# A two-layer decoder trunk on one core: two norm rows sent through DRAM on the GpSimd queue, and the last output block in two column halves

## The chip, the core and the metric

The kernel runs on one core of a Trainium2 chip. The time is the device time of one execution, in microseconds (us). Before the change it is 1134.34 us, the median of three runs (1133.87 to 1134.71).

## What is computed

A trunk of two layers over 512 tokens of width 1024, all in float32. Layer 0 mixes tokens by a forgetting attention (FoX), layer 1 by a latent attention (MLA) whose keys and values are computed from the stream after layer 0. Each layer ends in a squared-ReLU MLP of width 4096, and a last RMS norm closes the trunk:

```python
def rms_norm(x, g):
    y = x * lax.rsqrt(jnp.mean(x * x, axis=-1, keepdims=True) + EPS)
    return y * g

for layer in range(2):
    h = rms_norm(x, norm_mix_g[layer])
    x = x + (fox_mixer if layer == 0 else mla_mixer)(h, ...)
    h = rms_norm(x, norm_ffn_g[layer])
    x = x + jnp.square(jax.nn.relu(h @ w_up[layer])) @ w_down[layer]
    if layer == 0:
        k_nope, k_rope, v = mla_shared_kv(x, kv_norm_g, ...)
return rms_norm(x, final_norm_g)
```

## The kernel before, in words

**Tiling.** A stream `x` lies as 8 tiles of 128 features by 512 tokens. To keep float32 accuracy on TensorE, each operand is split into a high and a low part (`split`: ScalarE casts `hi`, VectorE subtracts to get `lo`) and each product is three matmuls (`three`). Weights come in pieces of 128x1024: a load into `raw` on SyncE's queue, a cast to `whi` on ScalarE, a subtraction to `wlo` on VectorE. Almost every operation is recorded through one helper, so most rows of the profile say L112, and tiles tell them apart.

**Order.** In the stages that matter here, TensorE, VectorE and ScalarE each carry out their instructions in exactly the order in which the code writes them (`order["on"]`). GpSimd (POOL) is not in that list; it has its own in-order stream. In the two MLPs (`ffn`) a table sets the order: `at(step, rank, fn)` files each piece of work under a step, and the steps are emitted one after another, by rank within a step.

**The norm's rows.** The norm's factor for each token, 1/sqrt(mean square), is computed once for 128 tokens by 4 blocks: `token_sums` on TensorE, two integer steps on VectorE, twelve small ones on POOL (`rsqrt_of`, L327 to L330). Tokens then lie on partitions. Where features lie on partitions, the factor is needed as a row of 512 tokens that is the same on all 128 partitions. `along_tokens` makes this with four float32 matmuls against an identity (`x8` in the profile, since each of them shows as two), and `rstd_tile` (L341) copies the result out of PSUM on ScalarE into a tile `rstd`. This happens three times: in the FoX stage (which the change leaves alone), in layer 0's MLP (`row`, L756, put at step 3; used only for the last 8 of 32 hidden blocks, `up_post`), and in MLA (L1158). There the row serves one multiplication, `u = krp * row` (L1165), whose result ScalarE rearranges (the two `copy` of 64 partitions at L1168). In ScalarE's order stand, behind these copies, the squares of the key-value latents (`square`, L1171 and L1176), whose sum over features is the next norm's `token_sums` (L1190) and, behind that, the chain of small VectorE steps `rsqrt_of(..., alone=True)` (L1194).

**The end.** The last MLP writes its output with tokens on partitions: for each of 4 blocks of 128 tokens and each of two halves of 512 features (`o`), `block_mm` (L1332) accumulates 24 matmuls in one PSUM bank; then the bank is scaled and added to the stream `xtok` (`add_to`, one VectorE operation). `o = 1` is done first for all blocks; when `o = 0` is added, `finish` (L1296) closes the block: the sum of squares on ScalarE (`activation` with `accum_out`), one VectorE operation that adds the two halves' sums, two integer operations and three Newton steps of two operations each on a 128x1 column (`fs`), and then both halves are scaled (`t` on VectorE, `u` on ScalarE) and stored by the queues of SyncE and ScalarE. For the last block nothing is left that could hide this chain.

Of the kernel before, what the change touches and what calls it, by code (L numbers as in the profile page):

```python
# [97 lines left out]
def trunk(ctx: ExitStack, tc: tile.TileContext, xT, wts, gains, fing, rope, out):  # L98
# [63 lines left out]
    def tt(shape=(P, S)):  # L162
        return tp_.tile(list(shape), F32, tag="t", name=nm("t"))
# [150 lines left out]
    def rsqrt_of(v, mult=1.0, alone=False, tags=("rs1", "rs2")):  # L314
        y, a = (small.tile([P, v.shape[-1]], F32, tag=t, name=nm("rs"), bufs=2 if t[:2] == "rs" else 1) for t in tags)

        nc.vector.tensor_single_scalar(a.bitcast(I32), v.bitcast(I32), 1, op=ALU.arith_shift_right)
        nc.vector.tensor_scalar(y.bitcast(I32), a.bitcast(I32), -1, RSQRT_BITS, op0=ALU.mult, op1=ALU.add)
        for step in range(3):
            m = mult if step == 2 else 1.0  # L320
            if alone:
                nc.vector.tensor_tensor(a, y, y, op=ALU.mult)
                nc.vector.scalar_tensor_tensor(out=a, in0=a, scalar=-0.5 * m, in1=v, op0=ALU.mult, op1=ALU.mult)
                nc.vector.scalar_tensor_tensor(out=y, in0=a, scalar=1.5 * m, in1=y, op0=ALU.add, op1=ALU.mult)
            else:

                nc.gpsimd.tensor_tensor(a, y, y, op=ALU.mult)  # L327
                nc.gpsimd.tensor_tensor(a, a, v, op=ALU.mult)
                nc.gpsimd.tensor_scalar(a, a, -0.5 * m, 1.5 * m, op0=ALU.mult, op1=ALU.add)
                nc.gpsimd.tensor_tensor(y, a, y, op=ALU.mult)  # L330
        return y
# [9 lines left out]
    def rstd_tile(r, tag="tp"):  # L341
        rb = along_tokens(r, tag)
        t = small.tile([P, S], F32, tag="rstd", name=nm("rstd"), bufs=2)
        nc.scalar.copy(t, rb)
        return t

    class Filler:
# [321 lines left out]
    def ffn(acc, layer, tokens, tail, begin):  # L669
# [8 lines left out]
        with ExitStack() as fs:  # L678
# [75 lines left out]
                nc.gpsimd.tensor_tensor(r2, rs, rs, op=ALU.mult)  # L754

            def row():  # L756
                norm["row"] = rstd_tile(norm["rs"], "go")

            def up_post(n):
                hf, j = divmod(n, HALF // P)  # L760
# [257 lines left out]
    with ExitStack() as mx:  # L1018
# [136 lines left out]
        prepare(KA + 4)  # L1155
        low_rank(ql[1], w[2][:4], hm, 0)
        low_rank(ql[2], w[2][4:], hm, 0)
        row = rstd_tile(rs)  # L1158
        prepare(KA + 5)


# [109 lines left out]
    fpool = ctx.enter_context(tc.tile_pool(name="fin", bufs=1, reuse_waits="tile"))  # L1271
    gfin = fpool.tile([P, D], F32, name="gfin")
    nc.scalar.dma_start(gfin, fing.partition_broadcast(P))
    nc.gpsimd.tensor_scalar(gfin, gfin, -1.0 / 8192, 0.0, op0=ALU.mult, op1=ALU.add)
    sums = fpool.tile([P, 2, NB], F32, name="sums")

    def turn_stream(at):
# [11 lines left out]
    def finish_first(tb):  # L1289
# [3 lines left out]
        nc.vector.tensor_scalar(sums[:, 1, tb : tb + 1], sums[:, 1, tb : tb + 1], 1.0 / D, EPS, op0=ALU.mult, op1=ALU.add)  # L1293
        nc.vector.tensor_tensor(xtok[tb][1], xtok[tb][1], gfin[:, S:], op=ALU.mult)

    def finish(tb):  # L1296

        junk = tt()
        nc.scalar.activation(out=junk, in_=xtok[tb][0], func=AF.Square, accum_out=sums[:, 0, tb : tb + 1])
        v, a, y = (small.tile([P, 1], F32, tag=f"fs{j}", name=nm("fs"), bufs=2) for j in range(3))  # L1300
        nc.vector.tensor_scalar(v, sums[:, 0, tb : tb + 1], 1.0 / D, sums[:, 1, tb : tb + 1], op0=ALU.mult, op1=ALU.add)
        nc.vector.tensor_single_scalar(a.bitcast(I32), v.bitcast(I32), 1, op=ALU.arith_shift_right)
        nc.vector.tensor_scalar(y.bitcast(I32), a.bitcast(I32), -1, RSQRT_BITS, op0=ALU.mult, op1=ALU.add)

        for m in (3.0, 12.0, 768.0):
            nc.vector.scalar_tensor_tensor(out=a, in0=y, scalar=v, in1=y, op0=ALU.mult, op1=ALU.mult)
            nc.vector.scalar_tensor_tensor(out=y, in0=a, scalar=-m, in1=y, op0=ALU.add, op1=ALU.mult)
        t, u = tt(), tt()
        nc.scalar.activation(out=u, in_=xtok[tb][1], func=AF.Copy, scale=y)
        nc.vector.scalar_tensor_tensor(out=t, in0=xtok[tb][0], scalar=y, in1=gfin[:, :S], op0=ALU.mult, op1=ALU.mult)  # L1310
        nc.scalar.dma_start(out[tb * P : (tb + 1) * P, S:], u)
        nc.sync.dma_start(out[tb * P : (tb + 1) * P, :S], t)

    def by_tokens(e, after, at, fn):

        s, los, quads, quad, w_cast, w_low, combine, add_to = (fn[n] for n in ("s", "los", "quads", "quad", "w_cast", "w_low", "combine", "add_to"))
        sh, sl, dn, lows = {}, {}, {}, []

        def hidden(k):
            return s[2 * CHUNKS + k // 4][:, k % 4, :]  # L1320

        def cast(k):
            sh[k] = rt()
            nc.scalar.copy(sh[k], hidden(k))

        def low(k):
            if k % 4 == 0:
                lows.append(fn["sp"].tile([P, 4, S], F32R, tag="s", name=nm("sl")))
            sl[k] = lows[-1][:, k % 4, :]
            nc.vector.tensor_tensor(sl[k], hidden(k), f32(sh[k]), op=ALU.subtract)  # L1330

        def block_mm(tb, o):  # L1332
            dn[tb, o] = bank(("up", "up", "go", "go")[tb])
            t = slice(tb * P, (tb + 1) * P)
            for i in range(4):
                for j in range(2):

                    k = i // 2 * 4 + j * 2 + i % 2
                    three(dn[tb, o], *los["w", o, i][j], sh[k][:, t], sl[k][:, t], i == 0 and j == 0, i == 3 and j == 1, flip=True)

        for k in range(KD):
            at(after + 1 + k // 2, 5, cast, k)
            at(e - 3 + k // 3, 2.5, low, k)
        for o in range(2):
            for i in range(4):
                m = ("w", o, i)
                hf, a = 2 * CHUNKS + i // 2, i % 2
                src = lambda hf=hf, a=a, o=o: quads[hf, a, o]
                due = e - 5 + i if o else e - 1 + i
                at(due - 4, 9, quad, hf, a, o)  # L1350
                at(due, 6, w_cast, m, src, i % 2 == 0 if o else i == 0)
                at(due + 1, 3, w_low, m, src)
        for n, (o, tb) in enumerate((o, tb) for o in (1, 0) for tb in range(NB)):
            at(e + n, 0, block_mm, tb, o)
            at(e + n + 1, 1, lambda tb=tb, o=o: add_to(tb, o, dn[tb, o]))
            if o == 0:
                at(e + 4 + tb // 2, 4, finish_first, tb)
                at(e + n + 1, 3.5, finish, tb)
        for j, part in enumerate(("u2", "u3", "c11", "c21", "v", "c12", "u4", "c22")):
            for b in range(2):  # L1360
                at(e + j // 2, 4, combine, b, part)
# [111 lines left out]
```

## Time and profile before

| | before |
|---|---|
| median of 3 runs | 1134.34 us (1133.87 to 1134.71) |
| the profiled execution: its time | 1133.68 us |
| its span, first to last instruction | 1131.9 us |
| granted TensorE clock | 0.999 |
| layer 0's MLP | about 261 to 599 us |
| MLA, from its first matmul to its output projection | about 599 to 786 us |
| layer 1's MLP and the end | about 786 us to the end |

The time of a run is longer than its span by what lies around it, 1.78 us in the profiled execution. The profile has the busy time of each engine, the chain of work that ended last (followed back from the end, each step to what released it), a timeline of the instructions with their start, length and the idle time before them, and groups of instructions by shape. In an instruction's name the tile before the arrow is written and the ones behind it are read.

### The profile page before, as it was taken

What the parts mean: (1) busy time and instruction counts of PE and PEld (TensorE: products, weight loads), DVE (VectorE), ACT (ScalarE), POOL (GpSimd) and SP (SyncE); (2) the same over time, 40 slices, a digit from 0 to 9 for tenths busy, and PEclk for the clock granted to TensorE, in tenths of its full rate; (3) what the DMA queues carried; (4) which work ended last, traced back from release to release, by engine and by line L of the source; (5) the groups of instructions that cost most, each with busy time, mean ns of one, the idle gap of its engine ahead of it and who ended that gap; (6) DMA issues with size and microseconds to landing.
All of it is one profiled execution on the core that took longest, in us unless ns stands there. A gap on an engine that the chain in (4) does not pass through costs nothing.

```text
span 1131.9 us, 14269 instructions
## 1 busy us (share of the span) xinstructions
PE 1114.8 (98%) x5340; PEld 910.8 (80%) x5340; DVE 780.6 (69%) x1420; ACT 581.7 (51%) x1060; POOL 19.7 (2%) x71
## 2 busy tenths in 40 slices
PE   8999999999999999999999999999999999999997
PEld 6777887788888888888888777788888888888885
DVE  6797888764567677577885877737256765765784
ACT  5565655644555454444454666635465544444622
POOL 1000000001000000000001100000100000000000
PEclk9999999999999999999999999999999999999999
DMA  5322222143724315311244211313442511611402
GB/s 189 132 94 92 77 75 75 57 147 96 278 95 149 112 38 171 108 57 56 98 144 137 79 41 52 112 56 97 159 173 67 183 67 56 191 62 42 135 1 75
DMA packets 36822, 116.66 MB, mean 103 GB/s; under 512 B 4224, under 2 KB 4864, under 8 KB 36752
## 3 DMA queue, kind: packets, MB, share of 16 engines
q1 hardware_dynamic: 35888, 114.15, 30.8%
q10 hardware_dynamic: 864, 1.60, 0.4%
q8 instruction: 42, 0.69, 0.2%
q14 instruction: 28, 0.23, 0.1%
HBM read 109.40 MB, written 6.32 MB: 102 GB/s over the span
## 4 chain that ended last, share of the span: by engine, by line
PE 91%; DVE 5%; ACT 2%; DMA 1%; issue 1%; POOL 0%; SPq 0%; ACTq 0%; DVEq 0%
PE up L112 35%; PE go L112 19%; PE acc L112 18%; PE sc L112 7%; PE tp L112 7%; PE keep L112 6%; DVE t L112 2%; DVE r L112 1%; ACT t L112 1%; DVE wlo L112 1%; DMA nb<-csc 0%; DMA t<-xT 0%; DVE ptl L112 0%; ACT whi L112 0%; ACT r L112 0%
## 5 line engine op out<-in xcount | busy, mean ns | idle before, releaser
L112 PE MATMUL acc<-r,whi 128*128 128x512 f32 x610 | 197.1, 403 | 5.4 <-ACT whi L112 4.8
L112 PE MATMUL up<-r,r 128*128 128x512 f32 x808 | 192.6, 390 | 0.0
L112 PEld LDWEIGHTS up<-r,r 128*128 128x128 f32 x808 | 151.2, 188 | 31.5
L112 PE MATMUL up<-r,whi 128*128 128x512 f32 x544 | 170.8, 390 | 0.0
L112 DVE TENSOR_TENSOR wlo<-raw,whi 128x1024 fp32r<-128x1024 f32 (+3 forms) x95 | 111.3, 1171 | 48.1 <-ACT whi L112 41.6
L112 DVE TENSOR_TENSOR t<-s,t 128x512 fp32r<-128x512 f32 x84 | 57.8, 688 | 121.9 <-ACT t L112 121.8
L112 PEld LDWEIGHTS acc<-r,whi 128*128 128x128 f32 x610 | 111.4, 190 | 31.1 <-ACT whi L112 5.1
L112 ACT CAST whi<-raw 128x1024 fp32r<-128x1024 f32 (+3 forms) x95 | 95.3, 1008 | 72.2 <-PE acc L112 33.0
L112 ACT ACTIVATE s<-up 128x512 f32<-128x512 f32 x56 | 33.4, 597 | 189.9 <-PE up L112 189.9
L112 PE MATMUL acc<-r,wlo 128*128 128x512 f32 x305 | 120.2, 394 | 0.1
L112 PEld LDWEIGHTS up<-r,whi 128*128 128x128 f32 x544 | 101.7, 188 | 20.9
L112 PE MATMUL up<-r,wlo 128*128 128x512 f32 x288 | 112.1, 389 | 0.0
L112 PE MATMUL go<-r,t 128*128 128x512 f32 x360 | 86.5, 389 | 0.0
L112 PE MATMUL sc<-r,r 128*128 128x512 f32 (+7 forms) x480 | 82.0, 357 | 2.4 <-ACT r L112 1.1
L112 PEld LDWEIGHTS go<-r,t 128*128 128x128 f32 x360 | 67.6, 188 | 14.0
L112 PE MATMUL go<-whi,t 128*128 128x512 f32 x240 | 78.7, 389 | 0.0
L112 PEld LDWEIGHTS sc<-r,r 64*128 64x128 f32 (+1 forms) x480 | 56.1, 186 | 26.8 <-issue 7.7
L112 PEld LDWEIGHTS acc<-r,wlo 128*128 128x128 f32 x305 | 57.6, 189 | 13.3 <-DVE wlo L112 0.4
L112 PEld LDWEIGHTS up<-r,wlo 128*128 128x128 f32 x288 | 54.1, 188 | 11.3
L112 DVE TENSOR_TENSOR r<-raw,r 128x512 fp32r<-128x512 f32 x72 | 46.5, 684 | 22.1 <-ACT r L112 22.1
L112 ACT ACTIVATE s<-s 128x512 f32<-128x512 f32 x64 | 40.5, 632 | 39.5 <-DVE s L112 37.8
L112 DVE TENSOR_TENSOR r<-q,r 128x512 fp32r<-128x512 f32 x94 | 60.4, 684 | 0.0
(199 smaller groups left out, 1859.7 us busy)
## 6 DMA issues: line engine op xcount, KB each, us to landing
raw<-wts SPq DMA_DIRECT2D x122, 512.0 KB, 3.6
q<-wts SPq DMA_DIRECT2D x56, 512.0 KB, 4.5
nb<-csc SPq DMA_DIRECT2D x8, 512.0 KB, 4.9
t<-xT SPq DMA_DIRECT2D x8, 256.0 KB, 5.8
r<-xT SPq DMA_DIRECT2D x8, 256.0 KB, 5.1
xmid<-r SPq DMA_DIRECT2D x8, 256.0 KB, 7.2
r<-xmid SPq DMA_DIRECT2D x8, 256.0 KB, 4.2
xkeep<-r SPq DMA_DIRECT2D x8, 256.0 KB, 2.1
```

The costliest lines, as they stand in the source:

```text
L112: ins = fn(*args, **kw)
```

## The change

Two of the three rows are no longer made by TensorE and ScalarE. A new helper sends the 512 factors to a line in DRAM by a DMA on the GpSimd queue (4 bytes for each partition and block), and reads that line back to all 128 partitions by a second one on the same queue, which waits for the first. In layer 0's MLP the row keeps its place in the table; in MLA it is issued as soon as the factors are there, two pieces earlier in the code than the matmuls stood.

In `finish`, the last block's `o = 0` half is accumulated in two banks of 256 columns each, one behind the other; each is added and squared by itself. For all blocks, the third Newton step is gone: the second step is one of third order (one operation more than a Newton step, so five in place of six), and the constant in `gfin` is adapted. The two squares' sums are added into the same column `sums[:, 1]`. `finish` moves behind `finish_first` in rank (3.5 to 4.5).

```diff
+    def row_by_dram(r):
+        line = keep.tile([S], F32, name=nm("line"))
+        real.gpsimd.dma_start(line.rearrange("(b p) -> p b", p=P), r)
+        t = small.tile([P, S], F32, tag="rstd", name=nm("rstd"), bufs=2)
+        real.gpsimd.dma_start(t, line.partition_broadcast(P))
+        return t
...
             def row():
-                norm["row"] = rstd_tile(norm["rs"], "go")
+                norm["row"] = row_by_dram(norm["rs"])
...
         rs = rsqrt_of(vx)
+        row = row_by_dram(rs)
         prepare(KA + 3)
...
         low_rank(ql[2], w[2][4:], hm, 0)
-        row = rstd_tile(rs)
         prepare(KA + 5)
...
+    def columns(tb, o):
+        return [slice(0, S)] if o or tb < NB - 1 else [slice(0, S // 2), slice(S // 2, S)]
+
+    def finish_squares(tb, n):
+        c = columns(tb, 0)[n]
+        nc.scalar.activation(out=tt()[:, c], in_=xtok[tb][0][:, c], func=AF.Square, accum_out=sums[:, 0, tb : tb + 1])
+        mean = sums[:, 1, tb : tb + 1]
+        nc.vector.tensor_scalar(mean, sums[:, 0, tb : tb + 1], 1.0 / D, mean, op0=ALU.mult, op1=ALU.add)
...
-        for m in (3.0, 12.0, 768.0):
-            nc.vector.scalar_tensor_tensor(out=a, in0=y, scalar=v, in1=y, op0=ALU.mult, op1=ALU.mult)
-            nc.vector.scalar_tensor_tensor(out=y, in0=a, scalar=-m, in1=y, op0=ALU.add, op1=ALU.mult)
+        nc.vector.scalar_tensor_tensor(out=a, in0=y, scalar=v, in1=y, op0=ALU.mult, op1=ALU.mult)
+        nc.vector.scalar_tensor_tensor(out=y, in0=a, scalar=-3.0, in1=y, op0=ALU.add, op1=ALU.mult)
+        nc.vector.scalar_tensor_tensor(out=a, in0=y, scalar=v, in1=y, op0=ALU.mult, op1=ALU.mult)
+        nc.vector.scalar_tensor_tensor(out=a, in0=a, scalar=-40.0 / 3, in1=a, op0=ALU.add, op1=ALU.mult)
+        nc.vector.scalar_tensor_tensor(out=y, in0=a, scalar=80.0, in1=y, op0=ALU.add, op1=ALU.mult)
...
         def block_mm(tb, o):
-            dn[tb, o] = bank(("up", "up", "go", "go")[tb])
             t = slice(tb * P, (tb + 1) * P)
-            for i in range(4):
-                for j in range(2):
-                    k = i // 2 * 4 + j * 2 + i % 2
-                    three(dn[tb, o], *los["w", o, i][j], sh[k][:, t], sl[k][:, t], i == 0 and j == 0, i == 3 and j == 1, flip=True)
+            dn[tb, o] = [bank(("up", "up", "go", "go", "up")[tb + n]) for n in range(len(columns(tb, o)))]
+            for c, dst in zip(columns(tb, o), dn[tb, o]):
+                for i in range(4):
+                    for j in range(2):
+                        k = i // 2 * 4 + j * 2 + i % 2
+                        w = [p[:, c] for p in los["w", o, i][j]]
+                        three(dst[:, c], *w, sh[k][:, t], sl[k][:, t], i == 0 and j == 0, i == 3 and j == 1, flip=True)
...
-            at(e + n + 1, 1, lambda tb=tb, o=o: add_to(tb, o, dn[tb, o]))
+            for j in range(len(columns(tb, o))):
+                at(e + n + 1, 1 + 2 * j, block_add, tb, o, j)
+                if o == 0:
+                    at(e + n + 1, 2 + 2 * j, finish_squares, tb, j)
...
-                at(e + n + 1, 3.5, finish, tb)
+                at(e + n + 1, 4.5, finish, tb)
```

What stands on GpSimd (POOL) in MLA, behind the last Newton step of the factors `rs`, before (the next factors, those of the query latent, follow at once):

```order
L327 TENSOR_TENSOR rs_5700<-rs_5699 128x4
L328 TENSOR_TENSOR rs_5700<-rs_5700,rs_5695 128x4
L329 TENSOR_SCALAR rs_5700<-rs_5700 128x4
L330 TENSOR_TENSOR rs_5699<-rs_5700,rs_5699 128x4
L327 TENSOR_TENSOR rs_6035<-rs_6034 128x4
```

and now, with the write of the line and the read of it to all partitions:

```order
L327 TENSOR_TENSOR rs_5697<-rs_5696 128x4
L328 TENSOR_TENSOR rs_5697<-rs_5697,rs_5692 128x4
L329 TENSOR_SCALAR rs_5697<-rs_5697 128x4
L330 TENSOR_TENSOR rs_5696<-rs_5697,rs_5696 128x4
L350 DMA line_5712<-rs_5696 128x4x1
L352 DMA rstd_5714<-line_5712 128x512
L327 TENSOR_TENSOR rs_6029<-rs_6028 128x4
```

Two DMAs have come in between two uses of POOL; nothing else on it has moved. What stands on TensorE in MLA, where the last query piece of the first half (`acc`) ends and the rotary keys (`sc`) begin, before:

```order
L112 MATMUL acc_5666<-r_5468,whi_5637 128x512
L112 MATMUL acc_5666<-r_5469,whi_5637 128x512
L112 MATMUL acc_5666<-r_5468,wlo_5638 128x512
L112 MATMUL tp_5776<-ident,rs_5699 128x128 x4
L112 MATMUL sc_5669<-r_5549,whi_5715 128x512
```

and now:

```order
L112 MATMUL acc_5663<-r_5454,whi_5634 128x512
L112 MATMUL acc_5663<-r_5453,wlo_5635 128x512
L112 MATMUL acc_5663<-r_5465,whi_5634 128x512
L112 MATMUL acc_5663<-r_5466,whi_5634 128x512
L112 MATMUL acc_5663<-r_5465,wlo_5635 128x512
L112 MATMUL sc_5666<-r_5546,whi_5716 128x512
```

The four matmuls against the identity are gone, and nothing has come in their place; the same holds for the four in layer 0's MLP, and for the ScalarE copy that followed each. What stands at the very end on VectorE, for the last block, before (`go` is the block's bank, `fs` the column of the Newton steps):

```order
L112 SCALAR_TENSOR_TENSOR r_7509<-go_10196,r_7630,r_7509 128x512
L112 TENSOR_SCALAR fs_10245<-sums 128x1
L112 TENSOR_SCALAR fs_10246<-fs_10245 128x1
L112 TENSOR_SCALAR fs_10247<-fs_10246 128x1
L112 SCALAR_TENSOR_TENSOR fs_10246<-fs_10247,fs_10245 128x1
L112 SCALAR_TENSOR_TENSOR fs_10247<-fs_10246,fs_10247 128x1
L112 SCALAR_TENSOR_TENSOR fs_10246<-fs_10247,fs_10245 128x1
L112 SCALAR_TENSOR_TENSOR fs_10247<-fs_10246,fs_10247 128x1
L112 SCALAR_TENSOR_TENSOR fs_10246<-fs_10247,fs_10245 128x1
L112 SCALAR_TENSOR_TENSOR fs_10247<-fs_10246,fs_10247 128x1
L112 SCALAR_TENSOR_TENSOR t_10257<-r_7509,fs_10247,gfin 128x512
```

and now, from the second half's add on (the first half's add, from `go`, and its mean stand ahead of these):

```order
L112 SCALAR_TENSOR_TENSOR r_7503<-up_10187,r_7624,r_7503 128x256
L112 TENSOR_SCALAR sums<-sums 128x1
L112 TENSOR_SCALAR fs_10263<-sums 128x1
L112 TENSOR_SCALAR fs_10264<-fs_10263 128x1
L112 SCALAR_TENSOR_TENSOR fs_10263<-fs_10264,sums 128x1
L112 SCALAR_TENSOR_TENSOR fs_10264<-fs_10263,fs_10264 128x1
L112 SCALAR_TENSOR_TENSOR fs_10263<-fs_10264,sums 128x1
L112 SCALAR_TENSOR_TENSOR fs_10263<-fs_10263 128x1
L112 SCALAR_TENSOR_TENSOR fs_10264<-fs_10263,fs_10264 128x1
L112 SCALAR_TENSOR_TENSOR t_10272<-r_7503,fs_10264,gfin 128x512
```

The add is half as wide, and five operations stand where six stood; the mean and the two integer operations are as many as before.

More of the change, by code (lines that the diff above doesn't have):

```diff
@@ L1273, in trunk @@
     nc.scalar.dma_start(gfin, fing.partition_broadcast(P))
-    nc.gpsimd.tensor_scalar(gfin, gfin, -1.0 / 8192, 0.0, op0=ALU.mult, op1=ALU.add)
+    nc.gpsimd.tensor_scalar(gfin, gfin, -3.0 / 256, 0.0, op0=ALU.mult, op1=ALU.add)
     sums = fpool.tile([P, 2, NB], F32, name="sums")
@@ L1294, in finish_first @@
         nc.vector.tensor_tensor(xtok[tb][1], xtok[tb][1], gfin[:, S:], op=ALU.mult)
+    def columns(tb, o):
[5 more added lines that the diff above has]
+        nc.vector.tensor_scalar(mean, sums[:, 0, tb : tb + 1], 1.0 / D, mean, op0=ALU.mult, op1=ALU.add)
     def finish(tb):
[L1298 to L1301, printed above, removed]
+        a, y = (small.tile([P, 1], F32, tag=f"fs{j}", name=nm("fs"), bufs=2) for j in range(2))
+        v = sums[:, 1, tb : tb + 1]
         nc.vector.tensor_single_scalar(a.bitcast(I32), v.bitcast(I32), 1, op=ALU.arith_shift_right)
         nc.vector.tensor_scalar(y.bitcast(I32), a.bitcast(I32), -1, RSQRT_BITS, op0=ALU.mult, op1=ALU.add)
-        for m in (3.0, 12.0, 768.0):
-            nc.vector.scalar_tensor_tensor(out=a, in0=y, scalar=v, in1=y, op0=ALU.mult, op1=ALU.mult)
-            nc.vector.scalar_tensor_tensor(out=y, in0=a, scalar=-m, in1=y, op0=ALU.add, op1=ALU.mult)
+        nc.vector.scalar_tensor_tensor(out=a, in0=y, scalar=v, in1=y, op0=ALU.mult, op1=ALU.mult)
[3 more added lines that the diff above has]
+        nc.vector.scalar_tensor_tensor(out=y, in0=a, scalar=80.0, in1=y, op0=ALU.add, op1=ALU.mult)
         t, u = tt(), tt()
@@ L1314, in by_tokens @@
     def by_tokens(e, after, at, fn):
-        s, los, quads, quad, w_cast, w_low, combine, add_to = (fn[n] for n in ("s", "los", "quads", "quad", "w_cast", "w_low", "combine", "add_to"))
+        s, los, quads, quad, w_cast, w_low, combine = (fn[n] for n in ("s", "los", "quads", "quad", "w_cast", "w_low", "combine"))
         sh, sl, dn, lows = {}, {}, {}, []
@@ L1332, in block_mm, with block_add @@
         def block_mm(tb, o):
-            dn[tb, o] = bank(("up", "up", "go", "go")[tb])
             t = slice(tb * P, (tb + 1) * P)
-            for i in range(4):
-                for j in range(2):
-                    k = i // 2 * 4 + j * 2 + i % 2
-                    three(dn[tb, o], *los["w", o, i][j], sh[k][:, t], sl[k][:, t], i == 0 and j == 0, i == 3 and j == 1, flip=True)
+            dn[tb, o] = [bank(("up", "up", "go", "go", "up")[tb + n]) for n in range(len(columns(tb, o)))]
[5 more added lines that the diff above has]
+                        three(dst[:, c], *w, sh[k][:, t], sl[k][:, t], i == 0 and j == 0, i == 3 and j == 1, flip=True)
+        def block_add(tb, o, n):
+            c = columns(tb, o)[n]
+            xt = xtok[tb][o][:, c]
+            nc.vector.scalar_tensor_tensor(out=xt, in0=dn[tb, o][n][:, c], scalar=fn["norm"]["r2"][:, tb : tb + 1], in1=xt, op0=ALU.mult, op1=ALU.add)
         for k in range(KD):
```

## The prediction

> **What bounds the kernel now.** I read the page first: busy times, then the shares of the chain that ended last.
>
> ```profile
> span 1131.9 us, 14269 instructions
> PE 1114.8 (98%) x5340; PEld 910.8 (80%) x5340; DVE 780.6 (69%) x1420; ACT 581.7 (51%) x1060; POOL 19.7 (2%) x71
> ...
> PE 91%; DVE 5%; ACT 2%; DMA 1%; issue 1%; POOL 0%; SPq 0%; ACTq 0%; DVEq 0%
> ```
>
> TensorE (PE) is busy for 98% of the span and holds 91% of the chain: what is taken from PE's stream shortens the run, unless something else ends at the same place. So the next view is the chain around the two removed rows, in order of time (start, length, what). First layer 0's MLP, then MLA:
>
> ```profile
> 267.65 16.49 PE up L112 x72
> 284.13 0.89 PE go L112 x8
> 285.02 15.00 PE up L112 x66
> ```
>
> ```profile
> 606.99 8.16 PE acc L112 x36
> 615.15 0.89 PE tp L112 x8
> 616.04 1.83 PE sc L112 x8
> ...
> 626.03 0.80 PE sc L112 x8
> ...
> 626.85 0.17 DVE rs L112
> ```
>
> Both rows stand in the chain with 0.89 us each, between matmuls that follow without a gap. In MLA the chain leaves PE at 626.83, where VectorE (DVE) begins the small steps of the next norm. The third place is the end, from the timeline (start, length, engine, instruction, idle time before it):
>
> ```profile
> 1123.51 0.40 PE L112 MATMUL go<-r,sl 128*128 128x512 f32 x1
> 1123.94 0.75 DVE L112 SCALAR_TENSOR_TENSOR r<-go,r,r 128x512 f32<-128x512 f32 x1 [1.34 <-PE go L112]
> 1124.73 0.63 ACT L112 ACTIVATE t<-r 128x512 f32<-128x512 f32 x1 [2.15 <-DVE r L112]
> ...
> 1125.48 0.21 DVE L112 TENSOR_SCALAR fs<-sums 128x1 f32<-128x1 f32 x1 [0.79 <-ACT t L112]
> 1125.73 0.34 DVE L112 TENSOR_SCALAR fs<-fs 128x1 int32<-128x1 int32 x2
> 1126.11 1.31 DVE L112 SCALAR_TENSOR_TENSOR fs<-fs,fs 128x1 f32<-128x1 f32 x6
> 1127.45 0.75 DVE L112 SCALAR_TENSOR_TENSOR t<-r,fs,gfin 128x512 f32<-128x512 f32 x1
> ```
>
> Every step waits for the one before; nothing runs beside them. From the last matmul's issue to `t` it is 3.94 us.
>
> **Layer 0's row.** PE loses 0.89 us. What could be late in its place is the next block's weights; their low part was written long before:
>
> ```profile
> 275.52 1.23 DVE L112 TENSOR_TENSOR wlo<-raw,whi 128x1024 fp32r<-128x1024 f32 x1 [4.66 <-ACT whi L112]
> 272.39 0.20 POOL L754 TENSOR_TENSOR r<-rs 128x4 f32<-128x4 f32 x1
> L112 DVE SCALAR_TENSOR_TENSOR s<-up,rstd x8: 682/691/692, 475.5 to 535.7; 128x512 f32<-128x512 f32 x8
> ```
>
> They end at 276.75 and are needed at 284.1. The factors are ready on POOL at 272.6 and the row is first read at 475.5: 203 us cover the two transfers, whatever they cost. On POOL nothing queues behind them until MLA. ScalarE (ACT) also loses its copy, off the chain. Gain: 0.89 us, and it moves all that follows by as much; I give MLA's times below as the trace has them, without this shift.
>
> **MLA's row.** PE again loses 0.89 us, but here the transfers have a deadline. The rows that set it:
>
> ```profile
> 606.55 1.25 DVE L112 TENSOR_TENSOR wlo<-raw,whi 128x1024 fp32r<-128x1024 f32 x1 [1.77 <-ACT whi L112]
> 606.82 1.04 POOL L330 TENSOR_TENSOR rs<-rs,rs 128x4 f32<-128x4 f32 x1
> 608.78 0.20 POOL L330 TENSOR_TENSOR rs<-rs,rs 128x4 f32<-128x4 f32 x1
> 610.61 1.23 DVE L112 TENSOR_TENSOR wlo<-raw,whi 128x1024 fp32r<-128x1024 f32 x1 [2.80 <-ACT whi L112]
> 616.56 1.05 ACT L112 CAST whi<-raw 128x1024 fp32r<-128x1024 f32 x1
> 618.78 0.68 DVE L112 TENSOR_TENSOR t<-sc,rstd 128x512 f32<-128x512 f32 x1
> 623.35 0.60 ACT L112 ACTIVATE t<-tp 128x512 f32<-128x512 f32 x1 [0.30 <-PE tp L112]
> 626.85 0.16 DVE L112 SCALAR_TENSOR_TENSOR rs<-sc,em 128x4 f32<-128x4 f32 x1 [0.19 <-PE sc L112]
> ```
>
> The factors are there at 608.98. `u = krp * row` ran at 618.78, and the next norm's steps began 8.07 us later, at 626.85. Of these 8.07 two idle times were PE's doing (ACT 0.30 before the second square, DVE 0.19 before the steps), so the work of ACT and DVE between them takes about 7.6 us. Without the row PE would let the steps begin at 626.85 - 0.89 = 625.96, so `u` must begin by 625.96 - 7.6 = 618.4. ACT and DVE can be ready: the cast at 616.56 stood behind the removed copy and can start about a microsecond earlier. So: landing by 618.4 (9.4 us after the factors) brings all of the 0.89; each us later takes one us away; at 619.3 the gain is gone and beyond it the run loses. Behind the waiting `u` stands all of DVE, and ACT's copies and squares behind `u`. Behind the two DMAs on POOL nothing is due until the query latent's factors. No load moves: SyncE's queue is as before.
>
> No DMA on POOL's queue is in the trace. The nearest rows (issue, queue, KB, median us to landing):
>
> ```profile
> csc<-t SPq DMA_DIRECT2D x1, 32.0 KB, 1.6
> cost<-rope SPq DMA_DIRECT2D x1, 256.0 KB, 2.5
> gsb<-gains ACTq DMA_DIRECT2D x1, 23.0 KB, 3.1
> nb<-csc SPq DMA_DIRECT2D x8, 512.0 KB, 4.9
> xmid<-r SPq DMA_DIRECT2D x8, 256.0 KB, 7.2
> ```
>
> At best the write costs what `csc` does (a store of a line to DRAM) and the read what `cost` does (256 KB to 128 partitions): 4.1 us. At worst both cost what the slowest group of stores does: 14.4 us. I take `gsb` for the write (many short rows) and `nb` for the read (a line of DRAM repeated to 128 partitions, if twice as long): 8.0 us, landing at 617.0. That is 1.4 us ahead of the deadline. The reserve is not wide: POOL's operations of 0.20 us took 1.04 once, beside DVE's operation at 606.55, and ended with it; another such operation, of 1.23 us, stands at 610.61, where POOL now works on the DMAs. One such stall gives 9.2 us, still in time.
>
> The Trainium skill ("DMA: Bandwidth & Descriptors", section Anatomy of one DMA) states about 2.0 us plus bytes over 436 GB/s for a DMA of this queue: 2.0 and 2.6 us here, an estimate of 4.6 us, which would leave the sum as it is. Against the change speaks a rule of the Trainium skill (same page, "DMA: Bandwidth & Descriptors", section Rules for kernel authors): a last dimension that isn't contiguous becomes one descriptor per element, 512 of them for a line of 2 KB. The page gives no time for that, and no run here shows it yet.
>
> **The last block in halves.** On PE, 24 matmuls of 512 columns become 48 of 256. Their pace, from the chain; the 256-column ones are FoX's value pieces, with tokens on the same side:
>
> ```profile
> 1112.70 11.22 PE go L112 x48
> 114.93 2.87 PE acc L112 x24
> ```
>
> 11.22/48 = 0.234 us against 2.87/24 = 0.120: 24 x 0.234 = 5.61 becomes 48 x 0.120 = 5.74, a loss of 0.13 us. The first half is complete 24 x 0.120 = 2.87 us ahead of the second; its add, square and mean (about 0.48 + 0.55 + 0.25 = 1.3 us) lie under the second half's matmuls, even behind the third block's `finish`, whose last operation on DVE ended at 1122.60 (the second half will end at about 1124.1):
>
> ```profile
> 1121.85 0.75 DVE L112 SCALAR_TENSOR_TENSOR t<-r,fs,gfin 128x512 f32<-128x512 f32 x1
> ```
>
> If that cover were gone, up to 0.8 us of add and square would be added back.
>
> What remains behind PE's end is priced by these groups (busy, mean ns):
>
> ```profile
> L112 DVE SCALAR_TENSOR_TENSOR v<-acc,rs,v 128x256 fp32r<-128x256 f32 x8 | 3.8, 480 | 3.3 <-ACT v L112 3.3
> L112 ACT ACTIVATE t<-t,sm 128x512 f32<-128x512 f32 x16 | 11.5, 718 | 3.4 <-DVE sm L112 3.4
> L112 ACT ACTIVATE t<-t,sm 128x256 f32<-128x256 f32 x16 | 8.0, 504 | 5.5 <-DVE sm L112 5.4
> ```
>
> The add falls from 0.75 to 0.48 (-0.27), the square as 718 to 504 ns (-0.21). One Newton operation less is (1127.45 - 1126.11)/6 = 0.22. Mean, integer steps, scaling and stores stay. Together -0.70 + 0.13 = -0.57 us. For the other blocks the shorter chain and the later rank lie under PE's matmuls and cost nothing.
>
> **The sum.** -0.89 - 0.89 - 0.57 = -2.35 us. The profiled execution's time is 1133.68 us (1131.9 and 1.78 around it), 0.66 below the median; I apply the difference to the median: 1134.34 - 2.35 = 1132.0 us. A measurement of this kernel can tell about 0.2%, 2.27 us, from no change: the forecast lies just on that line, at 1132.07.
>
> **Rivals.**
>
> - *MLA's row is late by little.* The two DMAs take 9.4 to 11.8 us together, for instance 10.3: then MLA's 0.89 is lost again and 1132.9 remains. For it: the two chained transfers and the stall seen on POOL. Against it: 9.4 us is more than any two rows but the stores' give. 0.26.
> - *MLA's row is so late that the run gets slower.* All three gains (2.35) are gone when the row lands at 618.4 + 2.35 = 620.75, 11.8 us after the factors. At 14.4 us it lands at 623.4: 5.0 us too late, 5.0 - 2.35 = +2.65, 1137.0 us. For it: 512 pieces of 4 bytes, which no row resembles, and the stores to DRAM at 7.2. Against it: those stores were eight at a time among weight loads, 256 KB each. A rule of the Trainium skill would lead here ("SBUF — State Buffer", section SBUF: two separate sides): VectorE and GpSimd share a port, and one can keep the other from writing a DMA's descriptors; the row at 606.82 agrees that they block each other. 0.07.
> - *The halves gain nothing.* PE at 256 columns could go at the pace of its weight loads, or the first half's chain sticks behind the third block's: then the end's 0.57 is lost, 1132.6 us. The value pieces' 0.120 us speaks against the first. 0.05.
>
> **How the numbers follow.** The forecast, row in time, 1132.0 us, has 0.62; its own range is 1131.3 to 1132.7, from 0.3 us each way in the end's terms and a run's spread of about 0.4. The late row reaches to 1134.3. From 1131.3 to 1134.3 all is held but the slow case and a few hundredths at each side. Faster by over 0.2% needs 1132.07 or less: about six tenths of the forecast's case, 0.38, and 0.04 from the edges of the others: 0.42. Slower by over 0.2% needs 1136.61, a landing 14.0 us after the factors or an unforeseen price of the new queue: 0.07. The rest, 0.51, is within.
>
> **What would show it.** In the new profile PE's `up` runs on without the 0.89 at 284 and `sc` follows `acc` at once in MLA; DVE's `t<-sc,rstd` names the weights' cast or PE before it, not the DMA, and the steps `rs` still follow PE's `sc`. At the end the last add is 0.48, the square some 0.42, and five `fs` operations stand ahead of `t`, about 3.4 us after the last matmul's issue. It is wrong if DVE waits for `rstd` by name, if the steps follow ACT or DVE in place of PE, if a gap opens on PE after either removed row, or if PE's last 48 matmuls take more than 6 us.

## The result, and the profile after

The changed kernel takes 1141.99 us (median of 4 runs, 1141.14 to 1143.35); the kernel before, run beside it, 1134.11 us (1133.46 to 1134.71). The ratio is 1.0071, 95% interval 1.0058 to 1.0083: slower by 7.9 us where 2.35 us were to be gained. The profiled execution took 1142.01 us; its span is 1140.2, 8.3 longer than before.

The page: TensorE's busy time rose by 3.3 us although 24 matmuls only were cut in two and 16 taken away, and in the chain DMA went from 1% to 3%.

```profile
span 1140.2 us, 14293 instructions
PE 1118.1 (98%) x5348; PEld 913.0 (80%) x5348; DVE 780.5 (68%) x1418; ACT 580.7 (51%) x1060; POOL 22.2 (2%) x75
...
PE 91%; DVE 3%; DMA 3%; ACT 2%; issue 1%; POOL 0%; SPq 0%; ACTq 0%; DVEq 0%; POOLq 0%
```

Layer 0's MLP went as forecast: in the chain `up` runs on where the 0.89 us of `go` stood (the `go` that is left is the token sums).

```profile
262.21 5.44 PE up L112 x24
267.65 0.79 PE go L112 x8
268.43 36.69 PE up L112 x161
```

In MLA the chain leaves TensorE for the two transfers. They stand there with 9.93 and 5.23 us (start, length, what):

```profile
609.18 0.21 POOL rs L330
609.38 0.28 issue
609.67 9.93 DMA line<-rs
619.60 0.29 issue
619.89 5.23 DMA rstd<-line
...
625.22 0.70 DVE t L112
...
630.97 1.84 PE sc L112 x8
```

The row's reader `u` (here `t<-sc,rstd`, since tiles share their names) begins at 625.22, 15.8 us after the factors (609.38). The timeline has the waits in brackets: VectorE stood idle for 7.55 us, then TensorE for 5.39, and the next norm's steps `rs` came without a wait on TensorE:

```profile
625.22 0.69 DVE L112 TENSOR_TENSOR t<-sc,rstd 128x512 f32<-128x512 f32 x1 [7.55 <-DMA rstd<-line]
...
630.97 1.84 PE L112 MATMUL sc<-ones,t 128*128 128x1 f32 x8 [5.39 <-DVE t L112]
632.84 0.16 DVE L112 SCALAR_TENSOR_TENSOR rs<-sc,em 128x4 f32<-128x4 f32 x1
```

The table by stretches (window, length, then busy time and instructions of PE, PEld, DVE, ACT, POOL, then the granted clock, the DMA share and GB/s) shows what the idle time brought with it: a clock of 0.50 and then 0.82.

```profile
625.00:630.00 5.00, 0.57 (x3) 0.15 (x1) 1.94 (x3) 3.96 (x7) 0.00 (x0) 1.00 0.05 6
630.00:635.00 5.00, 4.03 (x14) 3.58 (x15) 4.45 (x15) 3.54 (x6) 0.00 (x0) 0.50 0.21 76
635.00:640.00 5.00, 5.00 (x24) 4.19 (x23) 3.13 (x5) 1.65 (x3) 0.00 (x0) 0.82 0.33 107
```

The Trainium skill ("TensorE: Matmul & The Clock Gate", Part 1) says that an idle window of about 3.4 us halves TensorE's clock, and that a busy window as long restores it. The trace agrees with the first (0.50 behind 5.39 us of idle time). The return took longer here: 0.82 in the second stretch, if it is made of 0.50 and then 1.00, puts it at about 636.8, an estimated 5.8 us after TensorE went on.

The end went as forecast: add 0.48, square 0.42, five operations on `fs`, and from the last matmul's issue to `t` 3.13 us where it was 3.94. (The prediction's "about 3.4 us" there doesn't fit its own sum: 3.94 - 0.70 is 3.24.)

```profile
1132.56 0.28 PE L112 MATMUL up<-r,sl 128*128 128x256 f32 x1
1132.87 0.48 DVE L112 SCALAR_TENSOR_TENSOR r<-up,r,r 128x256 f32<-128x256 f32 x1 [0.44 <-PE up L112]
1133.44 0.42 ACT L112 ACTIVATE t<-r 128x256 f32<-128x256 f32 x1 [1.26 <-issue]
...
1135.50 0.16 DVE L112 SCALAR_TENSOR_TENSOR fs<-fs,fs 128x1 f32<-128x1 f32 x1
1135.69 0.75 DVE L112 SCALAR_TENSOR_TENSOR t<-r,fs,gfin 128x512 f32<-128x512 f32 x1
```

**Three stages, four marks.** To compare kernels, the timeline is cut at four instructions that all of them have: the token sums of layer 0's MLP, those of MLA, the second block of 24 matmuls in the last MLP, and the last block's `t`. The first three before, and in the changed kernel:

```profile
266.70 0.95 PE L112 MATMUL go<-ones,t 128*128 128x1 f32 x8
603.15 0.95 PE L112 MATMUL sc<-ones,t 128*128 128x1 f32 x8
792.11 5.75 PE L112 MATMUL up<-r,r 128*128 128x512 f32 x24
```

```profile
267.49 0.95 PE L112 MATMUL go<-ones,t 128*128 128x1 f32 x8
603.55 0.95 PE L112 MATMUL sc<-ones,t 128*128 128x1 f32 x8
801.39 5.75 PE L112 MATMUL up<-r,r 128*128 128x512 f32 x24
```

With `t` at 1127.45 and 1135.69 the stages take 336.45, 188.96 and 335.34 before, and 336.06, 197.84 and 334.30 after: -0.39, +8.88, -1.04. What stands ahead of the first mark varies by about 1.3 us between the profiles of this study (266.46 to 267.79), mostly in what the change doesn't touch, and is left out of these differences.

### The profile page after: what moved, and what is told of

It reads as the page before. It is cut to its first block, busy times and chain, and to the rows that moved or that the text cites. A ratio compares the mean times of both kernels' runs of the same rounds, so it can differ in the third digit from the quotient of the medians.

```text
span 1140.2 us, 14293 instructions
## 1 busy us (share of the span) xinstructions
PE 1118.1 (98%) x5348; PEld 913.0 (80%) x5348; DVE 780.5 (68%) x1418; ACT 580.7 (51%) x1060; POOL 22.2 (2%) x75
## 3 DMA queue, kind: packets, MB, share of 16 engines
q1 hardware_dynamic: 35888, 114.15, 31.1%
## 4 chain that ended last, share of the span: by engine, by line
PE 91%; DVE 3%; DMA 3%; ACT 2%; issue 1%; POOL 0%; SPq 0%; ACTq 0%; DVEq 0%; POOLq 0%
PE up L112 35%; PE go L112 18%; PE acc L112 18%; PE sc L112 8%; PE keep L112 6%; PE tp L112 6%; DVE t L112 1%; ACT t L112 1%; DMA line<-rs 1%; DMA raw<-wts 1%; DVE r L112 1%; ACT whi L112 1%; DVE wlo L112 1%; DMA rstd<-line 0%; DMA nb<-csc 0%
## 5 line engine op out<-in xcount | busy, mean ns | idle before, releaser
L112 PE MATMUL acc<-r,whi 128*128 128x512 f32 x610 | 199.7, 408 | 6.2 <-ACT whi L112 5.1
L112 PE MATMUL up<-r,r 128*128 128x512 f32 (+1 forms) x820 | 194.7, 389 | 0.0
L112 DVE TENSOR_TENSOR wlo<-q,whi 128x1024 fp32r<-128x1024 f32 x45 | 55.0, 1222 | 7.8 <-ACT whi L112 7.4
```

What stands on the lines that cost most here:

```text
L112: ins = fn(*args, **kw)
```

## The experiments

Two theories on the late row came first. P: the write is slow since it consists of 512 pieces of 4 bytes. Q: it is slow by its queue, the one of GpSimd. With them went a third question, what the idle TensorE costs beyond the wait. Then the runs themselves raised another one.

**e1: MLA's row by matmuls again.** The rest of the change stays.

```diff
         rs = rsqrt_of(vx)
-        row = row_by_dram(rs)
         prepare(KA + 3)
...
         low_rank(ql[2], w[2][4:], hm, 0)
+        row = rstd_tile(rs)
         prepare(KA + 5)
```

> The changed kernel with MLA's row made by matmuls and the copy again; layer 0's row by DRAM and the halved last block stay. If the late row in MLA is the whole of the loss (theory), the other two parts keep the gains forecast for them, 0.89 and about 0.6 us (the trace after shows 0.65 at the end): 1132.6 us, 1.5 below before, and u in MLA starts about 3.6 us after the matmuls against the identity, as before. If the new queue or the change elsewhere costs something of its own (rival), the time stays above 1134 us.

Measured: 1133.98 us, ratio 1.0000 (0.9992 to 1.0009). The loss is gone with MLA's transfers, so they made it. But the 1.5 us that the other two parts should have brought are not there. The stages are 336.01, 190.33, 334.30: MLA takes 1.37 us more than before with the same instructions in it.

**e2: MLA's transfers on SyncE's queue.**

```diff
-    def row_by_dram(r):
+    def row_by_dram(r, queue=real.gpsimd):
...
-        real.gpsimd.dma_start(line.rearrange("(b p) -> p b", p=P), r)
+        queue.dma_start(line.rearrange("(b p) -> p b", p=P), r)
...
-        real.gpsimd.dma_start(t, line.partition_broadcast(P))
+        queue.dma_start(t, line.partition_broadcast(P))
...
-        row = row_by_dram(rs)
...
         beside_piece(KA + 3)
+        row = row_by_dram(rs, real.sync)
```

> The changed kernel with MLA's two row transfers issued on SyncE's queue in place of POOL's, ahead of the load of the weight piece after next. If the new queue is what makes the write take 9.9 us (theory Q), the write takes 2 to 3.5 us and the read 3 to 5: landing about 615 to 618 us, in time, and the run takes 1131.7 to 1132.5 us. If 4-byte pieces into DRAM are slow on any queue (theory P), the write takes 8 us or more again, u waits for the row until after 622, and the run stays above 1137 us.

Measured: 1143.11 us, ratio 1.0076 (1.0064 to 1.0089). The DMA view (issue, queue, KB, us to landing) and SyncE's queue in the list of queues, which had 35888 packets in the change:

```profile
rstd<-line SPq DMA_DIRECT2D x1, 256.0 KB, 3.6
line<-rs POOLq DMA_DIRECT2D x1, 2.0 KB, 9.6
line<-rs SPq DMA_DIRECT2D x1, 2.0 KB, 12.3
```

```profile
q1 hardware_dynamic: 36560, 114.41, 31.9%
```

The write takes 12.3 us on this queue too, where it shares the way with weight loads. That speaks against Q, and e3, on GpSimd's queue, settles it. The 672 packets more fit 512 single elements and the read. e2's time is not the price of the late row alone: the weight load issued right behind the write stands in the chain with 13.19 us, where loads of weights before took 3.6 (the median of the 512 KB ones), and ScalarE waited for it ahead of `u`.

```profile
608.98 13.19 DMA raw<-wts
```

**e3: the line in 128 pieces of 16 bytes.** The four factors of a partition stand next to each other in DRAM.

```diff
-        real.gpsimd.dma_start(line.rearrange("(b p) -> p b", p=P), r)
+        real.gpsimd.dma_start(line.rearrange("(p b) -> p b", p=P), r)
```

> The changed kernel with both lines written in the order in which the factors lie, four of them (16 bytes) for each partition, so 128 pieces in place of 512; the rows then hold the factors in another order of tokens, so the result is not the reference's. If the number of pieces sets the write's time (theory P), it falls from 9.9 to about 3 to 5 us, u starts 5 to 7 us earlier, and the run takes 1132 to 1135 us. If the queue sets it whatever it carries (theory Q), the write stays at 8 us or more and the run at 1140 to 1142 us.

Measured: 1133.03 us, ratio 0.9992 (0.9983 to 1.0001).

```profile
rstd<-line POOLq DMA_DIRECT2D x2, 256.0 KB, 4.1
line<-rs POOLq DMA_DIRECT2D x2, 2.0 KB, 2.2
```

```profile
616.50 0.68 DVE L112 TENSOR_TENSOR t<-sc,rstd 128x512 f32<-128x512 f32 x1
...
625.31 0.16 DVE L112 SCALAR_TENSOR_TENSOR rs<-sc,em 128x4 f32<-128x4 f32 x1 [0.19 <-PE sc L112]
```

The same 2 KB on the same queue land in 2.2 us in place of 9.9, `u` waits for nothing, and the steps `rs` follow TensorE with the 0.19 us of before: P holds, and Q, by which the write would have stayed slow on this queue, falls. Number and size of the pieces change together here, so which of the two counts is not told apart. But the gain is some 0.9 us where the three parts should give 2.35: about 1.5 us are missing, as in e1.

**e4: TensorE kept busy during the wait.** 24 matmuls whose result nobody reads stand ahead of the sums that wait for the row (they write the PSUM bank that the next row overwrites).

```diff
+        rb = bank("tp")
+        for _ in range(24):
+            mm(rb, w[2][4][0], hm[4][0], start=True, stop=True)
         ss = token_sums(kv_acc, "sc")
...
-        krow = along_tokens(rs_kv)
+        krow = along_tokens(rs_kv, rb=rb)
```

> The changed kernel with 24 more matmuls on TensorE (into a bank that is overwritten later), where it idled for 5.4 us before the key-value norm's sums. If the drop of the granted clock to 0.50 behind that idle time is a part of the loss (theory), the sums take 0.8 in place of 1.84 us, the twelve matmuls behind them 2.7 in place of 4.8, and the run gets 2 to 3 us faster than the changed kernel: about 1139 to 1140 us. If only the late row counts (rival), the time stays at 1142 us, or grows by what the 24 matmuls delay.

Measured: 1141.82 us, ratio 1.0069 (1.0054 to 1.0084), with 1140.12 in the profiled execution and 1141.76 to 1142.28 in the others.

```profile
630.00:635.00 5.00, 4.12 (x22) 3.07 (x20) 4.31 (x15) 3.73 (x6) 0.00 (x0) 1.00 0.22 77
635.00:640.00 5.00, 4.75 (x26) 4.04 (x26) 4.67 (x8) 3.34 (x6) 0.00 (x0) 1.00 0.33 107
```

In the profile the clock stays at 1.00, and the times add up: `rs` starts 30.10 us behind MLA's token sums (632.91 - 602.81), 6.41 later than in e1 (626.99 - 603.30 = 23.69), and the stage is longer than e1's by 6.39 (196.72 - 190.33): all of it is the wait. In the change `rs` is 29.29 behind (632.84 - 603.55), 5.60 later than in e1, but the stage is longer by 7.51: the 1.91 us more are the slow clock's. The timed runs don't show such a gain: their median is 0.2 us below the change's, within the spread. The granted clock of the three other executions is 0.996, near the change's 0.994 to 0.996, where the profiled one has 0.998; so the slow clock probably came back in them, though no trace of them shows it. The 1.9 us hold for the profiled pair; what the clock costs on average stays open.

**What remained** was the 1.5 us missing in e1 and e3, with matmuls that nothing in the change touches running slower. One thing had moved them all: the shorter closing chain needs one small tile less, and all SBUF tiles allocated behind the pool of small tiles lie 64 bytes lower. Theory A: this is the cause. Theory B: something else in the change.

**e5: e1 at the old addresses.** Against e1, one small tile is widened, and nothing else. (The expectations of e5 to e7 count MLA between other marks, by which it takes 187.28 us before.)

```diff
-        a, y = (small.tile([P, 1], F32, tag=f"fs{j}", name=nm("fs"), bufs=2) for j in range(2))
+        a, y = (small.tile([P, n], F32, tag=f"fs{n}", name=nm("fs"), bufs=2)[:, :1] for n in (1, 16))
```

> The kernel of e1 (attention's row by matmuls, first MLP's row by DRAM, last block in halves) with one change that computes nothing: one of the two small tiles in finish is made 64 bytes wider in its two buffers together, so that every tile taken behind the pool of small tiles lies again at the SBUF address that it has in the kernel before. In e1 these tiles lie 64 bytes lower, since the closing chain has one small tile less. Theory A (the 1.4 us that e1 lost in unchanged matmuls come from those 64 bytes): the 72 matmuls of the output projection take 16.3 us again instead of 16.88, the attention stage 187.3 instead of 188.6, and the median falls from e1's 1133.98 to about 1132.7 (by the stages: 1134.1 - 0.46 - 0.65 = 1133.0 or a little less). Theory B (they come from something else in the change: the PSUM bank of the first MLP's row, the transfer, a shifted phase of the weight stream): 16.88, 188.6 and 1133.9 to 1134.1 as in e1.

**e6: the kernel before, 64 bytes lower.**

```diff
-        v, a, y = (small.tile([P, 1], F32, tag=f"fs{j}", name=nm("fs"), bufs=2) for j in range(3))
+        a, y = (small.tile([P, 1], F32, tag=f"fs{j}", name=nm("fs"), bufs=2) for j in range(2))
+        v = sums[:, 2, tb : tb + 1]
...
-    sums = fpool.tile([P, 2, NB], F32, name="sums")
+    sums = fpool.tile([P, 3, NB], F32, name="sums")
```

> The kernel before with nothing of the change but this: the last norm's variance v is kept in a third row of the tile sums instead of in a small tile of its own, which moves every tile taken behind the pool of small tiles 64 bytes lower, as the change did. Same instructions, same order, same waits. Theory A (addresses): the output projection's 72 matmuls take 16.9 us instead of 16.32, the attention stage about 188.6 instead of 187.28, the median 1135.0 to 1135.6, against 1134.1 before. Theory B (something else): no difference, 1134.1 within 0.2% of the kernel before and 16.32 for the projection.

Measured: e5 1133.06 us, ratio 0.9991 (0.9983 to 1.0000), nearer to 1132.7 of A than to 1134 of B; e6 1134.54 us, ratio 1.0007 (0.9998 to 1.0016), below the 1135.0 to 1135.6 of A. The times alone don't settle it. The output projection does, which A named as its sign: 16.32 us for its 72 matmuls in e5, as before, and 16.88 in e6, as in e1.

```profile
769.63 16.32 PE acc L112 x72
```

```profile
771.04 16.88 PE acc L112 x72
```

So do the stages: e5 335.50, 188.98, 334.74, so MLA is back to before within 0.02. And e6, with the kernel before's work, has MLA as slow as e1:

```profile
266.79 0.95 PE L112 MATMUL go<-ones,t 128*128 128x1 f32 x8
603.73 0.95 PE L112 MATMUL sc<-ones,t 128*128 128x1 f32 x8
794.05 5.75 PE L112 MATMUL up<-r,r 128*128 128x512 f32 x24
1128.10 0.75 DVE L112 SCALAR_TENSOR_TENSOR t<-r,fs,gfin 128x512 f32<-128x512 f32 x1
```

336.94, 190.32, 334.05: +0.49, +1.36, -1.29. The wider `sums` puts e6's last MLP only 32 bytes lower, and there it is faster, which A did not foresee and which keeps e6's median down. A holds: the place of the tiles is the cause. The groups show where the time sits, in single matmuls. MLA's largest group (count | busy us, mean ns | idle), before and then in e6:

```profile
L112 PE MATMUL acc<-r,whi 128*128 128x512 f32 x242 | 77.2, 399 | 0.6 <-DVE r L112 0.6
```

```profile
L112 PE MATMUL acc<-r,whi 128*128 128x512 f32 x242 | 78.3, 404 | 0.5 <-DVE r L112 0.5
```

**e7: the whole change with both faults mended.** It has e5's widened tile, e3's pieces, and the two readers (`u`, and the relu of layer 0's last hidden blocks in the same way) put the tokens back in order by reading the row with a stride of four elements.

```diff
-        return t
+        return t.rearrange("q (p b) -> q b p", p=P)
...
-        nc.vector.tensor_tensor(u, krp, row, op=ALU.mult)
+        nc.vector.tensor_tensor(u.rearrange("q (b p) -> q b p", p=P), krp.rearrange("q (b p) -> q b p", p=P), row, op=ALU.mult)
```

> The whole change with two corrections: the line is written in the order of the partitions (128 pieces of 16 bytes, as in e3) and the row's two readers on VectorE, u and the last chunk's relu, read it with a stride of four elements, which puts the tokens back in order; and the addresses are those of the kernel before, as in e5. Nothing is left out. Theory A with theory P (number of pieces sets the write's time): line 2.2 us, row 4.1 us as in e3, u by 616.6, attention stage 187.28 - 0.89 = 186.4, and with 0.46 in the first MLP and 0.65 at the end the median is 1134.1 - 2.0 = 1132.1. Theory B: as e3, 1133.0. If reading with a stride slows VectorE, u or the last chunk's relus take over their 0.69 us and that shows in the groups of lines 112 and of the relus; the attention stage then keeps its gain as long as u ends before 619.

Measured: 1131.88 us, ratio 0.9980 (0.9972 to 0.9989). The stages are 335.50, 188.08, 334.71: -0.95, -0.88, -0.63 against before, 2.46 in all where 2.35 were forecast. (The median fell by 2.1: the medians of e5, e7 and e11 give 0.4 to 0.6 less than their stages. In these three profiles the first mark itself is later, at 267.17 to 267.79 against 266.70, which is within the spread of that mark; whether it belongs to the change stays open.) The stride has a price, on VectorE only. These are the two readers here, and the same two before:

```profile
L112 DVE SCALAR_TENSOR_TENSOR s<-up,rstd 128x512 f32<-128x512 f32 x8 | 8.5, 1058 | 17.4 <-PE up L112 17.4
L112 DVE TENSOR_TENSOR t<-sc,rstd 128x512 f32<-128x512 f32 x1 | 1.0, 1048 | 0.0
```

```profile
L112 DVE SCALAR_TENSOR_TENSOR s<-up,rstd 128x512 f32<-128x512 f32 x8 | 5.5, 690 | 19.5 <-PE up L112 19.5
L112 DVE TENSOR_TENSOR t<-sc,rstd 128x512 f32<-128x512 f32 x1 | 0.7, 683 | 0.0
```

0.37 us each, under cover: `u` starts at 616.70 and the steps still follow TensorE.

**e8, e9, e10: is it the place within 128 bytes?** In the kernel before, the pools that the change moved start at a multiple of 128 bytes, but for the last MLP's, 32 past one; in e6 these came to a multiple and the stage got faster. Theory A2 takes the place within 128 bytes for what counts; A0 says that any move changes the time. e9 keeps two small numbers of before's closing chain in `sums`, e10 does so with another width; e8 is e7 with one number there. First e9 against before (e10 has [P, 8, NB] in its last line), then e8 against e7:

```diff
-        v, a, y = (small.tile([P, 1], F32, tag=f"fs{j}", name=nm("fs"), bufs=2) for j in range(3))
+        v, a = (sums[:, j, tb : tb + 1] for j in (2, 3))
+        y = small.tile([P, 1], F32, tag="fs0", name=nm("fs"), bufs=2)
...
-    sums = fpool.tile([P, 2, NB], F32, name="sums")
+    sums = fpool.tile([P, 10, NB], F32, name="sums")
```

```diff
-        a, y = (small.tile([P, n], F32, tag=f"fs{n}", name=nm("fs"), bufs=2)[:, :1] for n in (1, 16))
-        v = sums[:, 1, tb : tb + 1]
+        y = small.tile([P, 1], F32, tag="fs0", name=nm("fs"), bufs=2)
+        v, a = (sums[:, j, tb : tb + 1] for j in (1, 2))
...
-    sums = fpool.tile([P, 2, NB], F32, name="sums")
+    sums = fpool.tile([P, 8, NB], F32, name="sums")
```

> The kernel of e7 (the whole change, lines written in pieces of 16 bytes and read back with a stride) with every pool behind the small tiles at a multiple of 128 bytes, the last MLP's too: in e7, as in the kernel before, that MLP's pools begin 32 bytes past such a multiple, because the tile sums ahead of them has 32 bytes. Here one more small number moves into sums, and sums is padded to 128 bytes. Nothing is left out. Theory A2 (what counts is where an operand of TensorE starts within 128 bytes): the last stage, from the second block of the last MLP's up-projection to the last block's closing multiply, takes 334.71 in e7 and, as e6 with the same offset 0 was 1.29 shorter than before, about 333.4 here; the other two stages stay at 335.5 and 188.1; median 1130.6. Theory A0 (any other address would do as well or as badly; e6's shorter last stage came from elsewhere): 334.7 and 1131.9 as in e7.

> The kernel before with two small numbers of the last norm kept in sums, so that the pools of the first MLP and of the attention lie 128 bytes lower than before, at a multiple of 128 bytes again, and sums widened so that the last MLP's pools lie exactly where they did. Same instructions in the same order. Theory A2 (the place within 128 bytes counts): all three stages as before, 336.45, 188.96 and 335.34, median 1134.0 within 0.1%. Theory A0 (the address itself or any move counts): a move of 128 bytes costs what 64 did, first MLP about 336.9, attention about 190.3, median about 1135.3 at the last MLP's old place.

> The kernel of e9 with sums of another width, so that the last MLP's pools lie at a multiple of 128 bytes too (32 past it before). Nothing of the change is in it. Theory A2: the last stage 334.05 as in e6 instead of 335.34, the others as before, median 1132.7, a gain of 1.2 us without any change of the work. Theory A0: 335.3 and 1134.0 or more.

Measured: e8 1131.98 us, ratio 0.9985 (0.9976 to 0.9994); e9 1134.96, 1.0010 (1.0001 to 1.0019); e10 1133.88, 1.0001 (0.9992 to 1.0010). The stages, all worked out from the four marks, with the bytes by which the pools of the first two stages and of the last lie lower than before:

| | lower by (I, II / III) | I: MLP of layer 0 | II: MLA | III: last MLP, end |
|---|---|---|---|---|
| before | 0 / 0 | 336.45 | 188.96 | 335.34 |
| e6 | 64 / 32 | 336.94 | 190.32 | 334.05 |
| e9 | 128 / 0 | 337.26 | 189.47 | 335.35 |
| e10 | 128 / 32 | 337.26 | 189.42 | 334.08 |
| e5 (without MLA's row) | 0 / 0 | 335.50 | 188.98 | 334.74 |
| e7 (the change, mended) | 0 / 0 | 335.50 | 188.08 | 334.71 |
| e8 (the change, mended) | 128 / 32 | 336.40 | 188.57 | 333.70 |
| e1 (without MLA's row) | 64 / 64 | 336.01 | 190.33 | 334.30 |
| after | 64 / 64 | 336.06 | 197.84 | 334.30 |

A2 falls: 128 bytes lower is the same place within 128 bytes as before, and the first stage takes 0.81 us more there. Of A0 only so much holds that the address itself counts: a move of 128 bytes doesn't cost what 64 did (+0.81 and +0.51 in I and II, against +0.49 and +1.36). And the sizes repeat: the same addresses give the same stage within 0.05 us (e9 and e10 in I and II, e6 and e10 in III, before and e9 in III). A stage's time belongs to its addresses, and the parts of the change take their own times off it at each: I -0.95 at 0, -0.93 at 64 (e1 against e6), -0.86 at 128; II -0.88 at 0 and -0.85 at 128 (e8 against e10); III -0.60 and -0.63 at 0, but -0.38 at 32 lower. In stage III it is again single matmuls, here `r` with `r`, before and then in e10:

```profile
L112 PE MATMUL go<-r,r 128*128 128x512 f32 x40 | 12.6, 398 | 0.0
```

```profile
L112 PE MATMUL go<-r,r 128*128 128x512 f32 x40 | 12.3, 389 | 0.0
```

Both operands of this group are `r` tiles of the pool `rp`, which the kernel allocates ahead of the small tiles and which stayed where it was. So it is not the place of a matmul's own operands alone that counts; something that moved beside them does. What that is, which addresses are good, and by what mechanism, no run here shows.

**e11: each stage where it was shortest.** This tests whether a stage's time belongs to its addresses: it is e7 with `sums` in the pool of small tiles, so that stages I and II keep their old addresses and the last MLP lies 32 bytes lower.

```diff
-        a, y = (small.tile([P, n], F32, tag=f"fs{n}", name=nm("fs"), bufs=2)[:, :1] for n in (1, 16))
+        a, y = (small.tile([P, 1], F32, tag=f"fs{j}", name=nm("fs"), bufs=2) for j in range(2))
...
-    sums = fpool.tile([P, 2, NB], F32, name="sums")
+    sums = small.tile([P, 4, NB], F32, tag="sums", name="sums", bufs=1)
```

> The kernel of e7 (the whole change, lines in pieces of 16 bytes, read back with a stride), with each stage's pools where that stage was shortest in the runs so far: the first MLP's and the attention's at the addresses of the kernel before, the last MLP's 32 bytes lower, as in e6, e8 and e10. The tile sums moves from the last norm's pool into the pool of small tiles, whose size stays that of the kernel before. Nothing is left out. Theory R (a stage's time is fixed by the addresses of its own pools, and the three parts of the change take their own times off it): 335.5 as in e5 and e7, 188.1 as in e7, 333.7 as in e8; that is 1.3 less than e8 and 1.0 less than e7, so 1130.7 to 1131.0, 3.2 less than before. Theory S (the sum stays about the same, since what one stage saves another gives back, as e8 and e10 did beside e7 and before): 1131.9.

Measured: 1131.24 us, ratio 0.9971 (0.9959 to 0.9983), the fastest version of this study and faster than both kernels.

```profile
267.79 0.95 PE L112 MATMUL go<-ones,t 128*128 128x1 f32 x8
603.29 0.94 PE L112 MATMUL sc<-ones,t 128*128 128x1 f32 x8
791.44 5.75 PE L112 MATMUL up<-r,r 128*128 128x512 f32 x24
1125.13 0.75 DVE L112 SCALAR_TENSOR_TENSOR t<-r,fs,gfin 128x512 f32<-128x512 f32 x1
```

335.50, 188.15, 333.69, against 335.5, 188.1, 333.7 expected: R holds, within 0.07 us. The median is 0.2 us above the expected range; 0.6 us below e7 is less than the spread of each (1.5 and 1.4 us), so the stages carry that step, not the medians.

## Why the prediction was wrong

- **Layer 0's row, -0.89: right.** -0.95 at unchanged addresses (e5, e7). Its slow write (273.30 issued, the read at 283.57) lay under the 203 us of cover.
- **MLA's row, -0.89 if in time: the condition failed.** The deadline and its slope were right: with a row in time the stage gains 0.88 (e7), and in the change `rs` follows `u` by 7.62 us (632.84 - 625.22), where 7.6 were forecast. What failed is the step "I take `gsb` for the write (many short rows) and `nb` for the read": 3.1 + 4.9 = 8.0 us. The read took 5.23, near `nb`. The write took 9.93, three times `gsb`, and beyond the 7.2 that was taken for the worst. The gaps of 0.28 and 0.29 ahead of the two issues were not in the sum either, so the row was there 15.8 us after the factors instead of 8.0. The prediction had named the reason, "512 pieces of 4 bytes, which no row resembles", and still bounded it by rows of other kinds; its own slow rival, with 14.4 us as its worst price, had 0.07.
- **With the landing put right the working gives most of the time.** `u` at 625.22 is 0.40 later by the shift of MLA's token sums; without it 624.82, 6.42 behind the deadline of 618.4: -2.35 + 6.42 = +4.07 us. The three stages together lost 7.45. The rest, 3.4 us, is two prices that the prediction had not at all: the clock behind TensorE's idle 5.39 us, 1.9 in the profile (e4 against the change), and the addresses, +0.49 and +1.36 in the first two stages (e6) and about -0.44 in the last (-1.04 less the -0.60 of e5). 4.07 + 1.9 + 1.4 = 7.4. Two of these terms are remainders, the 1.9 and the -0.44, so their part in the sum is no test of them. The delay is tested: the working gives 6.42 - 0.89 = 5.53 us, and `rs` came 5.60 later than in e1.
- **The last block, -0.57: right** at unchanged addresses (-0.60 and -0.63; it was -0.38 at 32 bytes lower); the 256-column matmuls had the pace that the value pieces gave.
- **The rival of GpSimd's port** is not needed to explain the time: on SyncE's queue the write was no faster (12.3 us), and in 16-byte pieces it was fast on GpSimd's (2.2 us). "The halves gain nothing" fell with e5.

## What to carry to other kernels

A transfer is bounded by rows with its number and size of pieces, not with its bytes: 2 KB were 2.2 us in 16-byte pieces and 9.9 us in 4-byte ones, so lay the small side out in the order in which it stands on its partitions and undo the order at the reader, where it costs 0.37 us under cover. Before a matmul row is sent through DRAM, ask what TensorE does if it comes late: here 5.6 us of delay brought 1.9 us of slow clock with it in the profiled pair. And when a change frees or adds a tile, compare stages that it doesn't touch: if their matmuls changed pace, pad the tile away before judging the idea.

## What the runs showed of the hardware

- Writing 512 single elements of 4 bytes to DRAM took 9.6 to 11.0 us on GpSimd's queue and 12.3 on SyncE's; 128 pieces of 16 bytes took 2.2 to 2.5.
- With the same instructions, groups of TensorE's matmuls of 512 columns ran at 389 to 404 ns on average depending on where pools of tiles lie in SBUF: a move of some pools by 32 to 128 bytes changed a stage of 190 to 340 us by -1.3 to +1.4 us, and the same addresses gave the same stage within 0.07. One group (`go<-r,r`, 398 and 389 ns) changed though its own operands had not moved.
- A weight load issued on SyncE's queue right behind the write of 512 single elements took 13.19 us; the median of the 512 KB loads of the kernel before was 3.6.
- VectorE's 128x512 float32 operations with one operand read at a stride of four elements took 1048 to 1058 ns in place of 683 to 690.
- Behind 5.39 us of idle TensorE its granted clock was 0.50 in the next 5 us and 0.82 in the 5 after that.
